# One transpose for two heads in the recurrence, and the place of the half sums ahead of the feed-forward

## The chip, the cores and the metric

The kernel runs on one core of one Trainium2 chip. The metric is the device time of one execution in microseconds. Its engines work beside each other, each in the order of its own queue: TensorE (PE, with its weight loads PEld) multiplies and transposes, VectorE (DVE) and ScalarE (ACT) do elementwise work and read the results out of PSUM, GpSimd (POOL) does small work, and SyncE (SP) issues the transfers.

## The reference

One encoder layer is applied to 512 sample tokens and to 256 prompt tokens of width 1024. It is a mixer, a cross attention and a feed-forward, each with a norm before and after it and a residual:

```python
x = x + rms_norm(hybrid_mixer(rms_norm(x, p['g_mix_pre']), p), p['g_mix_post'])
m = rms_norm(mem, p['g_mem'])
x = x + rms_norm(cross_attention(rms_norm(x, p['g_x_pre']), m, p), p['g_x_post'])
h = rms_norm(x, p['g_ffn_pre'])
x = x + rms_norm(jnp.square(jax.nn.relu(h @ p['w_ff1'])) @ p['w_ff2'], p['g_ffn_post'])
```

Half of the mixer is a recurrence over the tokens (RWKV-7), with 8 heads of 64 and both directions; in each step a head's 64x64 state is decayed, corrected and extended:

```python
sa = jnp.einsum('bhij,bhj->bhi', S, -kk_t)
S = (S * w_t[:, :, None, :] + sa[..., None] * (kk_t * a_t)[:, :, None, :]
     + v_t[..., None] * k_t[:, :, None, :])
```

The other half is a gated linear attention in chunks of 64. All arithmetic is float32.

## The kernel before, in words

A float32 number is kept as a high part and a low part, and each product is made of three matmuls (high by high, high by low, low by high). split() (line 145) makes the two parts: ACT copies the high part, and DVE or POOL subtracts it from the number to get the low part. The 768 tokens are 6 tiles of 128.

**The recurrence.** Heads go in 4 pairs p; one head of a pair lies on partitions 0 to 63, the other on 64 to 127. The tokens are 12 chunks of 64, handled in 6 groups g of two chunks in each direction. products(st, g) (line 1001) is called for each pair and group, 24 times in all, and makes what does not depend on the state. It loads b_ (tile bkg), a_, tp and xv, makes the scores sa and sb on PE, masks them on DVE (lines 1021 to 1024), and then turns b_ over: for each of the two heads, four transposes of 64 rows by 128 columns (line 1028, PSUM tile bktp) and one ACT copy into bkt (line 1029). bkt lies in the tiles pl_hh, pl_hl and pl of the profile. PE multiplies it with the new values in line 1066.

step() (line 1035) is one step of the chain of states for two or three groups side by side: PE, ACT, PE, ACT, PE, DVE in turn. stage(q) (line 1160) places steps and the products for later steps beside each other, and the memory's keys and values (memory_block, line 1128, PE lines 249 and 1139) fill PE between them. The scores, bktp and the sums of finish() share the two PSUM banks of psm (line 75, tag "m").

**The passage to the feed-forward.** After the attention's output projection, channels_first(i) (line 1455) norms tile i (line 1458), transposes it (1462), and writes its high half on ACT (1465) and its low half on DVE (1466) into blk[j][l], the half j of the channels by the half l of the tokens (l = 0 is tiles 0 to 2, l = 1 is tiles 3 to 5). evacuate(i) (1434) and residual(i) (1445) come before it: DVE lines 1442 and 1450, ACT lines 1441 and 1452, POOL lines 1262 and 1264, and the stores of the new x to x2d.

The feed-forward multiplies blocks in Strassen's manner, with seven products of halves in place of eight for each of 8 slices f of 512 hidden channels. The right factors are, in the order of the products n, "21", "11", "t1", "t2", "22", "t3", "t4". "11" and the like are blocks as they stand; t1 to t4 are sums and differences of blocks. For these, both() (line 1594) first adds a block's high and low parts into an ordinary float32 tile (hsum, line 1596): four blocks in two parts q, eight instructions. Further differences (sub, line 1488) and splits (lines 149 and 150) follow. The left factors are weights: raw loads (w), sums of weights (ws, lines 1519 and 1488), and get() (line 1530), which makes the high part wh on ACT (1538) and the low part wl on DVE or POOL (1539). Line 1548 is the product on PE, into fz and fx. The order of the first products is slice 0 n 0 and 1, slice 1 n 0 and 1, slice 0 n 2 to 6, slice 1 n 2 to 6.

**What sets the order.** The program is written in the order of the code, and a planner (schedule_with_timeline_sim, line 1767) orders each engine's instructions before the run: of what is ready by its own model, that which has the highest priority, which is the place in the code unless tc.high_priority raises it. It hands out PSUM banks and tile buffers in the same pass. order_after(ins, prev) (line 43) tells it that one instruction must stand behind another, with no semaphore between them. Transfers are all issued by SP in order.

Of the kernel before, what the change touches and what calls it, by code (L numbers as in the profile page):

```python
# [10 lines left out]
AF = mybir.ActivationFunctionType  # L11
ALU = mybir.AluOpType
# [20 lines left out]
def kernel(ctx: ExitStack, tc: tile.TileContext, I, y_prompt, y_sample):  # L33
    nc = tc.nc
    act = nc.scalar
    dve = nc.vector
    pool = nc.gpsimd
    pe = nc.tensor
# [4 lines left out]
    def order_after(ins, prev):  # L43
        if prev is not None:
            tc.add_manual_dep(
                ins.ins,
                prev.ins.name,
                mybir.DependencyInfo(mybir.DependencyClass.NoSync, mybir.DependencyReason.DATA),
                reason="psum group order",
            )  # L50
        return ins

# [22 lines left out]
    def psm(name):  # L75
        return ps.tile([P, 512], F32, tag="m", bufs=2, name=name)
# [22 lines left out]
    ident = cp.tile([P, P], F32, name="ident")  # L99
# [28 lines left out]
    def fl(ap):  # L128
        return ap.rearrange("p a b -> p (a b)")
# [5 lines left out]
    HS = (slice(0, 64), slice(64, 128))  # L135
# [224 lines left out]
    def small_part(i, part):  # L360
# [6 lines left out]
        if part != 1:  # L367
# [7 lines left out]
                      in1=cv[:, col["mu_next"]:col["mu_next"] + 16], op=ALU.add)  # L375
# [112 lines left out]
    if True:  # L488
# [72 lines left out]
        with tc.high_priority(offset=3000):  # L561
            for p in range(4):
# [15 lines left out]
                for c0, n in SEQS:  # L578
                    pt, pz = psy("lops"), psy("gzps")
# [16 lines left out]
        for i in range(4):  # L596
# [3 lines left out]
            for k0 in range(0, KD, 4):  # L600
                pt = psm("ptr")
# [399 lines left out]
    def products(st, g):  # L1001

        p = st["p"]
        xv, a_, bkt, rbk, tp = places[g]
        b_ = mq1.tile([P, 4, 2, 64], F32, tag="bkg", bufs=3, name="bkg")
        dma(b_, bkd[p][:, g])
        for h, hs in enumerate(HS):
            dma(a_[hs, :, h:h + 2, :].rearrange("p u i x -> p u (i x)"), ard[p][hs, g])
        dma(tp, ttd[p][:, g])
        a, b = g, BACK[g]  # L1010
        for h in range(2):
            dma(xv[HS[1 - h], h].rearrange("p (d c) x -> p d (c x)", c=2),
                vtd[p][h][:, a:b + 1 if b > a else b - 1 if b else None:b - a])
        sa = psm("sca").rearrange("p (u x) -> p u x", u=4)
        sb = psm("scb").rearrange("p (u x) -> p u x", u=4)
        for u in range(4):
            pe.matmul(out=sa[64:128, u, :], lhsT=b_[0:64, u, 1, :], rhs=fl(a_[0:64, u, 0:2, :]), start=True, stop=True)
            pe.matmul(out=sb[0:64, u, :], lhsT=b_[64:128, u, 0, :], rhs=fl(a_[64:128, u, 1:3, :]), start=True, stop=True)
            pe.matmul(out=sa[0:64, u, 64:128], lhsT=b_[0:64, u, 0, :], rhs=a_[0:64, u, 1, :], start=True, stop=True)
            pe.matmul(out=sb[64:128, u, 0:64], lhsT=b_[64:128, u, 1, :], rhs=a_[64:128, u, 1, :], start=True, stop=True)  # L1020
        dve.tensor_tensor(out=u2(a_[64:128, :, 0, :]), in0=u2(sa[64:128, :, 0:64]), in1=bc2(m_strict[64:128]), op=ALU.mult)
        dve.tensor_tensor(out=u2(rbk[:, :, 0:64]), in0=u2(sa[:, :, 64:128]), in1=bc2(m_incl), op=ALU.mult)
        dve.tensor_tensor(out=u2(a_[0:64, :, 2, :]), in0=u2(sb[0:64, :, 64:128]), in1=bc2(m_strict[0:64]), op=ALU.mult)
        dve.tensor_tensor(out=u2(rbk[:, :, 64:128]), in0=u2(sb[:, :, 0:64]), in1=bc2(m_incl), op=ALU.mult)
        for h in range(2):
            pt = psm("bktp")[:, 0:256].rearrange("p (c x) -> p c x", c=4)
            for u in range(4):
                pe.transpose(out=pt[:, u, :], in_=fl(b_[HS[h], u]), identity=ident[HS[h], HS[h]])  # L1028
            act.activation(out=bkt[:, :, h, :], in_=pt, func=AF.Copy)

    def at_step(x, j):

# [170 lines left out]
    order = (4, 5, 6, 7, 0, 1, 2, 3)  # L1203
# [51 lines left out]
        return pd  # L1255

    CS = (slice(0, 512), slice(512, D))

    def rstd(sp, ss):

# [72 lines left out]
    with tc.tile_pool(name="ao", bufs=1, reuse_waits="tile") as ao:  # L1333
# [18 lines left out]
        for h in range(4):  # L1352
# [16 lines left out]
            for s_, (c0, n) in enumerate(SEQS):  # L1369
# [19 lines left out]
                for m in range(2):  # L1389
                    pt = psm("xt")  # L1390
# [4 lines left out]
                for e in range(2):  # L1395
# [3 lines left out]
                                     for m in range(2)])  # L1399
                    act.activation(out=oh[:, 2 * h + e, c0:c0 + n], in_=pm[:, 0:n], func=AF.Copy)  # L1400
                    dve.tensor_tensor(out=ol[:, 2 * h + e, c0:c0 + n], in0=pm[:, 0:n], in1=oh[:, 2 * h + e, c0:c0 + n],
                                      op=ALU.subtract)
# [5 lines left out]
        blk = [[[hb.tile([P, 4, 384], F32R, name=f"h{x}{j}{l}") for x in "hl"] for l in range(2)] for j in range(2)]  # L1408
        with tc.tile_pool(name="op2", bufs=1, reuse_waits="tile") as op2:
            wo2 = load_rows(op2, I["wo_x"][0], 1, range(KD))  # L1410

            def gain_half(name, half, tag):
                g_ = op2.tile([P, 512], F32, tag=tag, name="ghalf")
                dma(g_, I[name][:, CS[half]].broadcast_to([P, 512]))
                return g_

            g_post = [gain_half("g_x_post", 0, "gA"), gain_half("g_x_post", 1, "gB")]
            g_pre = [gain_half("g_ffn_pre", 0, "gC")]
            mo0, sums = [], []
            for i in range(6):  # L1420
                ts_ = slice(i * P, (i + 1) * P)
                pd = (psd, psy)[i % 2]("po")
                mm3(pd, [((oh[:, k, ts_], ol[:, k, ts_]), wo[k]) for k in range(KD)])
                ss = op2.tile([P, 2], F32, tag="ss2", bufs=6, name="ss2")
                mo = op2.tile([P, 512], F32, tag="mo0", bufs=6, name="mo0")
                with tc.high_priority():
                    act.activation(out=mo, in_=pd, func=AF.Square, scale=1.0 / 32, accum_out=ss[:, 0:1])
                    dve.tensor_tensor(out=mo, in0=pd, in1=g_post[0], op=ALU.mult)
                mo0.append(mo)
                sums.append(ss)  # L1430
            g_pre.append(gain_half("g_ffn_pre", 1, "gA"))
            mos, ress, rss = {}, {}, {}

            def evacuate(i):
                ts_ = slice(i * P, (i + 1) * P)
                res = ress[i] = op2.tile([P, D], F32, tag="res", bufs=2, name="res")
                dma(res, x1d[ts_, :])
                mo = mos[i] = mo0[i], op2.tile([P, 512], F32, tag="mo1", bufs=2, name="mo1")
                pd = (psd, psy)[i % 2]("po")
                mm3(pd, [((oh[:, k, ts_], ol[:, k, ts_]), wo2[k]) for k in range(KD)])  # L1440
                act.activation(out=mo[1], in_=pd, func=AF.Square, scale=1.0 / 32, accum_out=sums[i][:, 1:2])
                dve.tensor_tensor(out=mo[1], in0=pd, in1=g_post[1], op=ALU.mult)
                rss[i] = rstd(op2, sums[i])

            def residual(i):
                ts_ = slice(i * P, (i + 1) * P)
                mo, res = mos[i], ress[i]
                ss = op2.tile([P, 2], F32, tag="ss3", bufs=2, name="ss3")
                for half, cs in enumerate(CS):
                    dve.scalar_tensor_tensor(out=res[:, cs], in0=mo[half], scalar=rss[i], in1=res[:, cs], op0=ALU.mult, op1=ALU.add)  # L1450
                    dma(x2d[ts_, cs], res[:, cs])
                    act.activation(out=mo[half], in_=res[:, cs], func=AF.Square, scale=1.0 / 32, accum_out=ss[:, half:half + 1])
                rss[i] = rstd(op2, ss)

            def channels_first(i):
                mo, res = mos[i], ress[i]
                for half, cs in enumerate(CS):
                    dve.scalar_tensor_tensor(out=mo[half], in0=res[:, cs], scalar=rss[i], in1=g_pre[half],
                                             op0=ALU.mult, op1=ALU.mult)
                    pt = psm("ptr")  # L1460
                    for k in range(4):
                        pe.transpose(out=pt[:, k * P:(k + 1) * P], in_=mo[half][:, k * P:(k + 1) * P], identity=ident)
                    pt = pt.rearrange("p (k x) -> p k x", k=4)
                    hi, lo = (x[:, :, i % 3 * P:i % 3 * P + P] for x in blk[half][i // 3])
                    act.activation(out=hi, in_=pt, func=AF.Copy)
                    dve.tensor_tensor(out=lo, in0=pt, in1=hi, op=ALU.subtract)

            evacuate(0)
            for i in range(6):
                residual(i)  # L1470
                if i < 5:
                    evacuate(i + 1)
                channels_first(i)
# [12 lines left out]
    with tc.tile_pool(name="f1", bufs=1, reuse_waits="tile") as f1, tc.tile_pool(name="fw", bufs=1, reuse_waits="tile") as fw:  # L1486
# [98 lines left out]
        h = {"11": blk[0][0], "21": blk[1][0], "22": blk[1][1], "t1": blk[0][1]}  # L1585
# [3 lines left out]
        fl32 = {}  # L1589
        for q in range(2):  # L1590
            ks = slice(2 * q, 2 * q + 2)
            for ij, (j, l) in {"12": (0, 1), "11": (0, 0), "22": (1, 1), "21": (1, 0)}.items():
                fl32[ij, q] = stage_tile({"12": "a", "11": "b", "22": "c", "21": "d"}[ij] + str(q), "hsum")
        def both(q, ij, j, l):
            ks = slice(2 * q, 2 * q + 2)
            dve.tensor_tensor(out=fl32[ij, q], in0=blk[j][l][0][:, ks, :], in1=blk[j][l][1][:, ks, :], op=ALU.add)
        def halves_of(t, q, src, lo_eng):
            ks = slice(2 * q, 2 * q + 2)
            split(h[t][0][:, ks, :], h[t][1][:, ks, :], src, lo_eng)
# [18 lines left out]
        for at, (f, n) in enumerate(jobs):  # L1618
# [29 lines left out]
            if n in (1, 4, 5):  # L1648
                u = st[{1: "11", 4: "12", 5: "22"}[n]]
# [121 lines left out]
```

## Time and profile before

| | us |
|---|---|
| median of 3 timed runs | 1554.85 |
| the three runs | 1558.52, 1554.85, 1549.77 |
| the profiled execution | 1548.75 |
| its span, first to last instruction | 1546.6 |
| PE busy on the transposes of bktp (192) | 21.8 |
| DVE on the sums of the halves (8), mean of one | 0.95 |

A row of the timeline gives the start and length in us, the engine, the line, the operation, what it writes and reads, the shape and the number of instructions; in square brackets stands how long the engine was idle before it and what ended that wait. A row of the groups gives the same without a start, then the busy time in us and the mean of one in ns, then the idle time before them. Matmuls overlap, so their lengths don't add up; what one takes from the queue is seen in the starts of its neighbours.

### The profile page before, as it was taken

Reading aid. Unit: us, or ns where it says so; the run is one execution under the profiler, and the core shown is the slowest. Engines: PE = TensorE matmul, PEld = TensorE weight load, DVE = VectorE, ACT = ScalarE, POOL = GpSimd, SP = SyncE. Lnnn points to the kernel's source line nnn. Section 1 sums busy time; section 2 is a strip of 40 time slices with the busy share of each in tenths; the row PEclk is TensorE's granted clock in tenths of the full one; section 3 lists DMA queues with packets and bytes.
Section 4 is the critical chain, followed back from the end, with each engine's and each line's share of the span. In section 5 each row is a group of like instructions: output and inputs, shape, how many; then the busy total and the mean of one; then the engine's idle time right before and its main releaser. Section 6 shows DMA issues by size and latency. Waiting matters only on the chain.

```text
span 1546.6 us, 27578 instructions
## 1 busy us (share of the span) xinstructions
PE 1408.3 (91%) x10238; PEld 1183.6 (77%) x10238; DVE 1076.7 (70%) x1913; ACT 706.0 (46%) x1477; POOL 220.9 (14%) x304
## 2 busy tenths in 40 slices
PE   7998899897799987999699999978999999999996
PEld 6886778775676766777478887868999998787785
DVE  5555896698567994866665554279766667788886
ACT  5664345443423442344353454345554555454342
POOL 5301000000000000003211233320000002132132
PEclk9999899987779996799799999988999999999998
DMA  6687666584468667464452332244554547555334
GB/s 165 177 314 210 171 197 156 167 228 102 128 187 232 180 184 168 106 166 144 128 179 98 107 100 79 82 154 155 196 170 153 181 157 291 155 175 172 120 103 136
DMA packets 279562, 250.30 MB, mean 162 GB/s; under 512 B 89264, under 2 KB 227059, under 8 KB 279428
## 3 DMA queue, kind: packets, MB, share of 16 engines
q1 hardware_dynamic: 279428, 248.54, 53.8%
q8 instruction: 81, 1.33, 0.4%
q14 instruction: 53, 0.43, 0.1%
HBM read 164.11 MB, written 82.58 MB: 160 GB/s over the span
## 4 chain that ended last, share of the span: by engine, by line
PE 59%; DVE 13%; DMA 11%; issue 8%; SPq 3%; ACT 3%; POOL 2%; DVEq 0%; ACTq 0%; POOLq 0%
PE pd L249 19%; PE fx L1548 7%; PE gx L1548 6%; PE fz L1548 5%; PE gz L1548 5%; SPq L41 3%; PE po L249 3%; DMA wraw<-in_w_in_dram 1%; DVE ws L1488 1%; PE hsum L639 1%; DVE wl L1539 1%; DMA raw<-in_w_out_dram 1%; PE xo L249 1%; POOL rs L1264 1%; PE bktp L1028 1%
## 5 line engine op out<-in xcount | busy, mean ns | idle before, releaser
L249 PE MATMUL pd<-hT_hi,whi 128*128 128x256 f32 (+1 forms) x512 | 183.5, 358 | 9.1 <-DVE gd L327 4.1
L249 PE MATMUL pd<-hT_lo,whi 128*128 128x256 f32 (+1 forms) x512 | 180.2, 352 | 0.3 <-DVE hT_lo L208 0.3
L249 PE MATMUL pd<-hT_hi,wlo 128*128 128x256 f32 (+1 forms) x512 | 178.5, 350 | 0.0
L149 ACT ACTIVATE whi<-wraw 128x256 fp32r<-128x256 f32 x192 | 77.5, 415 | 97.2 <-PE pd L249 59.4
L249 PEld LDWEIGHTS pd<-hT_hi,whi 128*128 128x128 f32 x512 | 100.9, 197 | 24.0 <-DVE gd L327 4.0
L150 DVE TENSOR_TENSOR wlo<-wraw,whi 128x256 fp32r<-128x256 f32 x192 | 80.2, 437 | 48.2 <-ACT whi L149 46.6
L249 PEld LDWEIGHTS pd<-hT_lo,whi 128*128 128x128 f32 x512 | 101.0, 197 | 13.1 <-DVE hT_lo L208 0.5
L249 PEld LDWEIGHTS pd<-hT_hi,wlo 128*128 128x128 f32 x512 | 100.2, 196 | 13.2 <-issue 0.5
L150 DVE TENSOR_TENSOR ul<-ur,uh 128x768 fp32r<-128x768 f32 x56 | 75.3, 1351 | 30.2 <-ACT uh L149 17.7
L149 ACT ACTIVATE uh<-ur 128x768 fp32r<-128x768 f32 x56 | 47.2, 845 | 106.6 <-PE gz L1548 51.8
L1538 ACT ACTIVATE wh<-w 128x1024 fp32r<-128x1024 f32 x64 | 67.1, 1053 | 36.7 <-PE fz L1548 24.2
L1539 DVE TENSOR_TENSOR wl<-w,wh 128x1024 fp32r<-128x1024 f32 x56 | 68.2, 1217 | 15.3 <-ACT wh L1538 14.7
L1548 PE MATMUL gx<-wh,uh 128*128 128x512 f32 x192 | 74.9, 397 | 4.2 <-DVE acc L1741 4.2
L1548 PE MATMUL gx<-wl,uh 128*128 128x512 f32 x192 | 75.9, 395 | 0.0
L1548 PE MATMUL gx<-wh,ul 128*128 128x512 f32 x192 | 75.4, 395 | 0.0
L1539 POOL TENSOR_TENSOR wl<-w,wh 128x1024 fp32r<-128x1024 f32 x8 | 20.9, 2610 | 329.3 <-ACT wh L1538 329.3
L1548 PE MATMUL fz<-hh,wh 128*128 128x384 f32 x192 | 66.1, 344 | 1.7 <-ACT wh L1538 1.7
L1548 PE MATMUL fz<-hl,wh 128*128 128x384 f32 x192 | 65.9, 343 | 0.0
L1548 PE MATMUL fz<-hh,wl 128*128 128x384 f32 x192 | 65.2, 344 | 0.6 <-DVE wl L1539 0.6
L1538 ACT ACTIVATE wh<-ws 128x1024 fp32r<-128x1024 f32 x48 | 50.5, 1052 | 27.2 <-PE fx L1548 22.5
L1548 PE MATMUL gz<-wl,uh 128*128 128x512 f32 x144 | 56.9, 395 | 0.0
L249 PE MATMUL pd<-mem_hi,wlo 128*128 128x512 f32 x128 | 56.0, 439 | 0.9 <-DVE wlo L150 0.9
(537 smaller groups left out, 3980.4 us busy)
## 6 DMA issues: line engine op xcount, KB each, us to landing
w<-in_w_ff_dram SPq DMA_DIRECT2D x64, 512.0 KB
ur<-ud SPq DMA_DIRECT2D x56, 384.0 KB
wraw<-in_w_in_dram SPq DMA_DIRECT2D x108, 128.0 KB
ud<-u SPq DMA_DIRECT2D x32, 384.0 KB
ud<-us SPq DMA_DIRECT2D x24, 384.0 KB
wraw<-in_wkv_x_dram SPq DMA_DIRECT2D x64, 128.0 KB
lora<-lo_t SPq DMA_DIRECT2D x20, 384.0 KB
bkg<-bkd SPq DMA_DIRECT2D x24, 256.0 KB
```

The source lines that it names most:

```text
L41: return nc.sync.dma_start(out=out, in_=in_)
L149: act.activation(out=hi, in_=src, func=AF.Copy)
L150: (lo_eng or pool).tensor_tensor(out=lo, in0=src, in1=hi, op=ALU.subtract)
L249: pe.matmul(out=out, lhsT=a, rhs=b, start=(i == 0), stop=(i == n - 1))
L639: pe.matmul(out=pt[:, 0:n], lhsT=ones_bd, rhs=src[:, c0:c0 + n], start=True, stop=True)
L1028: pe.transpose(out=pt[:, u, :], in_=fl(b_[HS[h], u]), identity=ident[HS[h], HS[h]])
L1264: pool.tensor_tensor(out=rs, in0=ms, in1=neg_half, op=ALU.pow)
L1488: dve.tensor_tensor(out=out, in0=a, in1=b, op=ALU.subtract)
L1538: act.activation(out=hi, in_=t[name], func=AF.Copy)
L1539: lo_eng.tensor_tensor(out=lo, in0=t[name], in1=hi, op=ALU.subtract)
L1548: pe.matmul(out=out, lhsT=a, rhs=b, start=first and i == 0, stop=last and i == n - 1, skip_group_check=True)
```

## The change

In products() the two heads' transposes become one of all 128 rows for each u, into the whole PSUM tile, and one copy takes the place of two. In the passage to the feed-forward the last instruction of line 1466 is remembered, and each of the eight sums of line 1596 is told to stand behind it on DVE. As channels_first goes through the tiles in order, what is remembered is the low half of the last tile's second half of channels. The words given as a reason are renamed.

```diff
-        for h in range(2):
-            pt = psm("bktp")[:, 0:256].rearrange("p (c x) -> p c x", c=4)
-            for u in range(4):
-                pe.transpose(out=pt[:, u, :], in_=fl(b_[HS[h], u]), identity=ident[HS[h], HS[h]])
-            act.activation(out=bkt[:, :, h, :], in_=pt, func=AF.Copy)
+        pt = psm("bktp").rearrange("p (u x) -> p u x", u=4)
+        for u in range(4):
+            pe.transpose(out=pt[:, u, :], in_=fl(b_[:, u]), identity=ident)
+        act.activation(out=bkt.rearrange("p u h x -> p u (h x)"), in_=pt, func=AF.Copy)
...
+    last_lo = [None]
...
-                    dve.tensor_tensor(out=lo, in0=pt, in1=hi, op=ALU.subtract)
+                    last_lo[0] = dve.tensor_tensor(out=lo, in0=pt, in1=hi, op=ALU.subtract)
...
-            dve.tensor_tensor(out=fl32[ij, q], in0=blk[j][l][0][:, ks, :], in1=blk[j][l][1][:, ks, :], op=ALU.add)
+            order_after(dve.tensor_tensor(out=fl32[ij, q], in0=blk[j][l][0][:, ks, :], in1=blk[j][l][1][:, ks, :],
+                                          op=ALU.add), last_lo[0])
```

More of the change, by code (lines that the diff above doesn't have):

```diff
@@ L48, in order_after @@
                 mybir.DependencyInfo(mybir.DependencyClass.NoSync, mybir.DependencyReason.DATA),
-                reason="psum group order",
+                reason="order",
             )
```

## The prediction

> **What bounds the kernel now.** I read the page first, then stage tables for the two places that the change touches, then the timelines, groups and waits there.
>
> ```profile
> span 1546.6 us, 27578 instructions
> ## 1 busy us (share of the span) xinstructions
> PE 1408.3 (91%) x10238; PEld 1183.6 (77%) x10238; DVE 1076.7 (70%) x1913; ACT 706.0 (46%) x1477; POOL 220.9 (14%) x304
> ```
>
> TensorE (PE) is busy for 91% of the span. So an edit pays where it shortens PE's own queue, or where PE stands waiting. The stage tables show one place of each kind; the columns are stage, length, busy time of PE, weight loads, VectorE (DVE), ScalarE (ACT) and GpSimd, then granted clock, DMA share and GB/s.
>
> ```profile
> 430.00:760.00 330.00, 297.22 (x3772) 228.26 (x3770) 239.52 (x628) 121.20 (x333) 14.55 (x29) 0.87 0.62 167
> 600.00:630.00 30.00, 27.15 (x366) 22.56 (x364) 22.39 (x72) 7.17 (x23) 0.00 (x0) 0.50 0.68 174
> 1031.00:1050.00 19.00, 6.74 (x24) 4.98 (x24) 16.51 (x22) 8.48 (x15) 1.72 (x4) 0.58 0.64 204
> 1050.00:1081.00 31.00, 28.36 (x141) 27.79 (x140) 31.00 (x33) 15.85 (x22) 0.00 (x0) 0.87 0.36 110
> ```
>
> The recurrence, where all 24 calls of products() run, is 430 to 760: PE works 297.22 of 330 us (90%), so time taken from its queue there is mostly worth its face value. The passage from the last norm to the feed-forward is 1031 to 1050: PE works 6.74 of 19 us while DVE works 16.51. From 1050 to 1081 DVE works every microsecond and PE loses another 2.6 us. So the passage belongs to DVE.
>
> **Part 1, the transposes.** Gone are 192 transposes of 64 rows and 48 evacuations of 128x256; new are 96 transposes of 128 rows and 24 evacuations of 128x512. The nearest row for the new transpose is line 1139, which moves four 128x128 blocks in the same stretch. The start of the next group in the timeline gives what each takes from the queue.
>
> ```profile
> 474.88 0.56 PE L1028 MATMUL bktp<-ident,bkg 64*128 64x64 f32 x8
> ...
> 690.22 0.47 PE L1028 MATMUL bktp<-ident,bkg 64*128 64x64 f32 x8
> 690.62 0.50 PE L249 MATMUL pd<-mem_hi,wlo 128*128 128x512 f32 x1
> ...
> 706.52 0.66 PE L1139 MATMUL kvt<-ident,mo 128*128 128x128 f32 x4
> 707.11 0.32 PE L1046 MATMUL rec<-pl_hh 64*64 64x64 f32 x2
> 707.36 0.46 PE L1028 MATMUL bktp<-ident,bkg 64*128 64x64 f32 x4
> 707.75 0.45 PE L1077 MATMUL rec<-pl 128*64 128x64 f32 x8
> ```
>
> One head's four transposes take 707.75 - 707.36 = 0.39 us of the queue, so a pair done one head after the other takes 0.78. Eight in one group take 690.62 - 690.22 = 0.40: there the heads overlapped. The new group takes 707.11 - 706.52 = 0.59. So a product whose heads stand apart gains 0.19 us, and one whose heads overlap loses 0.19. In PE's timeline three of the 24 products overlap like this (the first at 474.88, the last at 690.22); in the others the heads stand apart or run one after the other. That makes 21 x 0.19 - 3 x 0.19 = 3.4 us less in PE's queue; times the 90%, 3.1 us.
>
> The Trainium skill (TensorE: Matmul & The Clock Gate, Part 3: Packing small matmuls) says that matmuls on different row groups of the array run at the same time, and the two heads sit on rows 0 to 63 and 64 to 127. By that rule all 24 products would overlap already, part 1 would be 0.9 x 24 x 0.19 = 4.1 us lost, and the sum below 1555.95. The groups of eight agree with it; the groups of four show that the heads rarely stand side by side in the queue.
>
> ```profile
> L1029 ACT ACTIVATE pl_hh<-bktp 128x256 f32<-128x256 f32 x16 | 5.8, 384 | 8.6 <-PE bktp L1028 8.1
> ...
> L1142 ACT ACTIVATE mo<-kvt 128x512 f32<-128x512 f32 x8 | 4.8, 596 | 2.3 <-PE kvt L1139 2.2
> ```
>
> ```profile
>   PEld rec L1051: 1.3, 3
>   PEld sca L1017: 1.0, 2
>   PEld rec L1066: 0.8, 1
>   PEld bktp L1028: 0.7, 1
> ```
>
> On ACT, 48 x 0.384 = 18.4 us become 24 x 0.596 = 14.3 us. ACT works 121 of 330 us there, so those 4.1 us are hidden behind PE either way; if ACT were the bound they would come on top. The second fence is what PE's weight loads waited for behind line 1029 (us in total, times): 3.8 us. Its last row is the second head waiting for the first head's evacuation, which goes for good (0.7). The others stay: the last copy is now 0.596 - 0.384 = 0.21 us longer, but there is one instead of two. I take 0.7 of the 3.8. Fewer holds on the two "m" banks could shorten PE's waits for DVE's reads of sca and scb; I count nothing for that, since those waits end when DVE has read the scores, before any transpose. Sum of part 1: 3.1 + 0.7 = 3.8, of which I keep 3.0, because some PE time freed inside a recurrence step only uncovers the next wait of that step. Bounds: all heads apart and all waits gone, 24 x 0.19 + 3.8 = 8.4 us gained; all heads overlapped already, 24 x 0.19 = 4.6 us lost.
>
> **Part 2, the sums of the halves.** The eight sums of line 1596 may stand on DVE only behind the last tile's last low half (line 1466). Before, six stood ahead of it:
>
> ```profile
> 1030.87 0.95 DVE L1596 TENSOR_TENSOR hsum<-hh,hl 128x768 f32<-128x768 f32 x1
> 1031.74 0.69 DVE L1466 TENSOR_TENSOR hl<-ptr,hh 128x512 fp32r<-128x512 f32 x1
> 1032.34 2.68 DVE L1596 TENSOR_TENSOR hsum<-hh,hl 128x768 f32<-128x768 f32 x3
> ...
> 1039.96 1.41 DVE L1458 SCALAR_TENSOR_TENSOR mo<-res,rs,ghalf 128x512 f32<-128x512 f32 x2 [1.22 <-POOL rs L1264]
> 1042.61 0.69 DVE L1466 TENSOR_TENSOR hl<-ptr,hh 128x512 fp32r<-128x512 f32 x1 [1.24 <-ACT hh L1465]
> 1043.34 1.83 DVE L1596 TENSOR_TENSOR hsum<-hh,hl 128x768 f32<-128x768 f32 x2
> 1045.08 0.69 DVE L1466 TENSOR_TENSOR hl<-ptr,hh 128x512 fp32r<-128x512 f32 x1
> ...
> 1049.15 1.22 DVE L1539 TENSOR_TENSOR wl<-w,wh 128x1024 fp32r<-128x1024 f32 x1
> ```
>
> Back to back one takes 0.87 us (1031.74 - 1030.87), so 6 x 0.87 = 5.2 us leave the last norm's path: four stand ahead of that tile's evacuation and residual, two before its last low half. What PE then waits for is the first weights' low half (line 1539, 1049.15):
>
> ```profile
> 1050.42 0.69 PE L1548 MATMUL fz<-hh,wl 128*128 128x384 f32 x1 [0.21 <-DVE wl L1539]
> ...
> 1075.40 0.69 PE L1548 MATMUL fx<-t2h,wl 128*128 128x384 f32 x1 [2.43 <-DVE wl L1539]
> ```
>
> PE's first products could start up to 5.2 us sooner. The weight loads move too: SyncE issues them in order behind the last tile's two stores to x2d, which wait for the residual that the four sums delay by 4 x 0.87 = 3.5 us; so the raw weights come that much sooner and don't take the cover away. But the 5.2 us come back on DVE after the norm, where it has no free time until 1081, and behind them stand the sums' own users (the products with t1 to t4) and the weights' splits. If all that DVE does before the wait at 1075.40 ends is needed by then, PE only waits more there and the gain is nothing; if the norm's gaps, so far filled by sums, stay empty besides, it is a loss. The norm's two idle gaps in the fence (1.22 and 1.24) are 2.5 us together; doubled, the loss is 2.5. If DVE could put off what is not yet due, the gain is 5.2 plus PE's waits of 2.43 and 0.21: 7.8 us. Work that is not yet due stands there:
>
> ```profile
> 1060.31 1.21 DVE L1488 TENSOR_TENSOR ws<-w,w 128x1024 f32<-128x1024 f32 x1
> 1061.44 0.95 DVE L150 TENSOR_TENSOR t3l<-hsum,t3h 128x768 fp32r<-128x768 f32 x1
> 1062.31 1.21 DVE L1519 TENSOR_TENSOR ws<-w,w 128x1024 f32<-128x1024 f32 x1
> ```
>
> The two weight sums are the second slice's (each slice has one of line 1519, and this is the second), used from the tenth product on; t3 is used in the eighth; PE is at its sixth at 1075. These three alone are 3.4 us. Whether the planner puts them behind can't be seen in this trace, so I take 3 us, a little under the middle of 0 and 7.8, because the loss of 2.5 is open too.
>
> **Sum.** The profiled execution took 1548.75 us, its span of 1546.6 and 2.15 around it; 1548.75 - 3.0 - 3.0 = 1542.75. The median of the three timed runs is 1554.85, 6.1 above that execution; carried onto it, the forecast is **1548.85**.
>
> **The rivals.**
>
> *Both gains come nearly whole* (0.27). Heads apart almost everywhere and waits gone, 5 us; DVE puts off what isn't due, 7.8 us. 1554.85 - 12.8 = 1542.05. For it: PE's queue is the bound at both places. Against it: DVE is full for 31 us.
>
> *Nothing is saved* (0.16). The heads overlap in most products and DVE hands the 5.2 us back: 0.9 x 4.6 = 4.1 us lost, nothing gained, 1558.95. For it: a group of eight takes as long as a group of four, and DVE is full. Against it: only three of 24 products show such a group.
>
> *A bare wait in the recurrence* (0.12), the case of slower. The order of the engines is planned afresh, and the products' PE and ACT work is what stands between the steps and the loads.
>
> ```profile
> 586.38 0.21 PE L796 MATMUL merge<-tdz,lsb 32*32 32x32 f32 x2 [4.21 <-DMA tdz<-td]
> ```
>
> Here PE stood 4.21 us for a transfer, and from 600 to 630 the clock was 0.50. At half clock the 27.15 us worked there would have been 13.6 at full clock. One more such place costs 4.2 + 13.6 = 17.8 us; less the 6 gained, 1554.85 + 11.8 = 1566.65. It decides as soon as one wait of over 4 us stands in the recurrence that wasn't there. The Trainium skill (TensorE: Matmul & The Clock Gate, Part 1) gives about 3.4 us as the window after which an idle PE falls to half clock; the 4.21 us wait and the 0.50 agree with it. For this rival: PE's queue is in order, so a merge placed too early holds all that stands behind it. Against it: a shorter queue of products frees banks and ACT rather than binding them.
>
> **How the numbers follow.** The forecast has 0.45, with its own range from 1544 to 1555. A measurement of this kernel can tell about 0.5% (7.8 us) from no change, so faster means under 1547.1 and slower over 1562.6. Faster: the first rival's 0.27 and 0.11 of the forecast's, 0.38. Slower: the last rival, 0.12. Within: 0.50. The range goes down to 1538, where parts 1 and 2 at their best bounds (8.4 + 7.8 = 16.2 under the median) put it, and up to 1561.5, which takes in the second rival and a further 2.5 us lost on DVE, and leaves out most of the last rival.
>
> **What would show it.** Right: PE's transposes of bktp become 24 groups of 0.66 us, 16 us in all; ACT's on line 1029 to 14.3; all eight sums stand behind the last line 1466, which ends near 1040.5 if the recurrence kept its length; line 1548 takes up its wl products some 5 us sooner after the last out-projection, and DVE's waits in front of it grow between the fourth and the seventh product. Wrong: the feed-forward's continuous stretch begins as late after the last out-projection as before; the recurrence's length moves by over 8 us either way, which would be its new order and not the transposes; or its clock changes.

## The result, and the profile after

| | before | after |
|---|---|---|
| median, us (18 runs each) | 1554.93 | 1564.72 |
| lowest and highest | 1548.71 to 1567.42 | 1558.04 to 1570.67 |
| profiled execution | 1548.75 | 1566.52 |
| its span | 1546.6 | 1564.6 |

The change makes the kernel slower: the ratio is 1.0053, with a 95% interval of 1.0032 to 1.0074, some 8 us. Two numbers have to be kept apart. The profiled execution of before lies 6 us under that kernel's median, the one of after 2 us above its own. So differences between the two traces show where time went, but their sum, 18 us, is about twice what the medians show; sizes are taken from the ratios.

The page of after, to hold against the page lines of before:

```profile
span 1564.6 us, 27338 instructions
...
PE 1408.3 (90%) x10142; PEld 1182.4 (76%) x10142; DVE 1079.6 (69%) x1913; ACT 701.0 (45%) x1453; POOL 224.5 (14%) x304
```

PE's busy time is 1408.3 us in both kernels. Nothing is worked longer; PE stands idle longer. The stages of after, with the passage to the feed-forward shifted by 19 us, because the last output projection ends at 1049.0 in place of 1030.1 (same columns as in the prediction):

```profile
430.00:760.00 330.00, 289.29 (x3558) 222.51 (x3557) 235.85 (x610) 111.34 (x294) 18.09 (x29) 0.86 0.60 164
600.00:630.00 30.00, 28.03 (x480) 23.06 (x479) 18.23 (x58) 10.64 (x29) 0.00 (x0) 0.89 0.75 187
680.00:730.00 50.00, 38.23 (x536) 31.13 (x536) 19.04 (x52) 10.74 (x26) 0.00 (x0) 0.55 0.48 124
1050.00:1069.00 19.00, 8.18 (x30) 6.53 (x31) 16.99 (x23) 9.37 (x16) 1.69 (x4) 0.58 0.78 250
1069.00:1100.00 31.00, 27.59 (x145) 26.96 (x144) 31.00 (x32) 15.69 (x21) 0.00 (x0) 0.93 0.30 93
```

In the recurrence PE works 289.29 of 330 us, 8 less than before; the half clock that stood at 600 to 630 is gone from there (0.89) and stands at 680 to 730 (0.55). The passage is much as it was. So the loss lies in the recurrence, and both parts of the change did what they say. The groups of bktp in after (count, then shortest, median and longest in ns, first and last start):

```profile
L1027 PE MATMUL bktp<-ident,bkg x96: 270/273/476, 441.6 to 754.9; 128*128 128x128 f32 x96
L1028 ACT ACTIVATE pl_hh<-bktp x8: 592/597/597, 442.8 to 717.5; 128x512 f32<-128x512 f32 x8
```

The transposes are 96 of 128 rows, and a copy takes 0.597 us, as forecast from line 1142. The sums in after, on DVE:

```profile
1058.34 0.69 DVE L1466 TENSOR_TENSOR hl<-ptr,hh 128x512 fp32r<-128x512 f32 x1 [0.16 <-ACT hh L1465]
1058.95 7.03 DVE L1596 TENSOR_TENSOR hsum<-hh,hl 128x768 f32<-128x768 f32 x8
1065.89 1.22 DVE L1539 TENSOR_TENSOR wl<-w,wh 128x1024 fp32r<-128x1024 f32 x1
```

and what PE then waits for:

```profile
1067.16 0.69 PE L1548 MATMUL fz<-hh,wl 128*128 128x384 f32 x1 [4.63 <-DVE wl L1539]
```

All eight sums stand behind the last low half, in one block of 7.03 us, and the first weights' low half stands behind all of them: PE waits 4.63 us for it where it waited 0.21.

Where does the recurrence lose its time? SP's queue shows it. Before, the rows of the third pair's inverses and join (td<-snf is a store of the inverses, tdz<-td what the join loads from it, sxf<-ld the load for the fourth pair's inverses):

```profile
576.72 0.83 SPq L41 DMA_DIRECT2D td<-snf  x1
...
579.51 2.14 SPq L41 DMA_DIRECT2D td<-snf  x1
...
590.26 1.04 SPq L41 DMA_DIRECT2D tdz<-td  x1
...
602.50 0.71 SPq L41 DMA_DIRECT2D sxf<-ld  x1
```

After:

```profile
576.05 0.33 SPq L41 DMA_DIRECT2D td<-snf  x1
...
582.31 0.88 SPq L41 DMA_DIRECT2D tdz<-td  x2
...
601.36 0.46 SPq L41 DMA_DIRECT2D td<-snf  x1
...
602.92 1.41 SPq L41 DMA_DIRECT2D sxf<-ld  x1
...
606.70 0.91 SPq L41 DMA_DIRECT2D tdz<-td  x2
```

The second store goes out at 601.36 in place of 579.51. DVE had its data ready at 578.3, as before (578.5). The copy that makes it, before and after:

```profile
577.33 1.12 DVE L760 COPY snf<-sqf 48x1024 f32<-48x1024 f32 x1
```

```profile
577.23 1.08 DVE L760 COPY snf<-sqf 48x1024 f32<-48x1024 f32 x1
```

In after the store stands behind 11 transfers that are a weight's and the join's own, to 585.7, and then behind 21 others, 13 of them loads for later products(). The join's second half needs it, and its results lie in the tile (sqf) that the fourth pair's inverses clear first. PE's second half of the join and DVE's first step of the fourth pair's inverses, before:

```profile
592.71 0.94 PE L796 MATMUL merge<-tdz,lsb 32*32 32x32 f32 x46 [0.78 <-DMA tdz<-td]
```

```profile
613.11 0.19 DVE L752 TENSOR_TENSOR stmp<-sqf,snf 112x31 f32<-112x31 f32 x1
```

and after:

```profile
610.03 1.66 PE L796 MATMUL merge<-tdz,lsb 32*32 32x32 f32 x48 [1.43 <-DMA tdz<-td]
```

```profile
626.91 0.18 DVE L752 TENSOR_TENSOR stmp<-sqf,snf 112x31 f32<-112x31 f32 x1
```

The inverses then end at 673 in place of 646, and the fourth pair's join and all of the recurrence that hangs on it come later. The later start is 14 of these 27 us. The other 13 are length: between the inverses' first and last step DVE does 24.3 us of other work in the new order, where it did 15.0. On the way stands a wait that is much easier to see. SP sends a result of the late inverses (sxf) at 685.95; ACT's square in finish() reuses that buffer; PE stands behind ACT:

```profile
685.95 0.78 SPq L41 DMA_DIRECT2D qd<-sxf  x1
```

```profile
690.87 0.84 ACT L1105 ACTIVATE fb<-ya 128x768 f32<-128x768 f32 x1 [10.73 <-DMA qd<-sxf]
```

```profile
691.77 2.93 PE L639 MATMUL hsum<-fb,ones_bd 128*128 128x512 f32 x4 [11.25 <-ACT fb L1105]
```

No wait points at the store: from 579 to 601, where the loss begins, PE's longest is 2.62 us, shorter than the 4.21 us in the same place before. The waits of the recurrence show only the loss's end.

### The profile page after: what moved, and what is told of

Its sections match the earlier page's. It is cut to its first block, busy times and chain, and to the rows that moved or that the text cites. A ratio compares the mean times of both kernels' runs of the same rounds, so it can differ in the third digit from the quotient of the medians.

```text
span 1564.6 us, 27338 instructions
## 1 busy us (share of the span) xinstructions
PE 1408.3 (90%) x10142; PEld 1182.4 (76%) x10142; DVE 1079.6 (69%) x1913; ACT 701.0 (45%) x1453; POOL 224.5 (14%) x304
## 4 chain that ended last, share of the span: by engine, by line
PE 59%; DVE 16%; DMA 8%; issue 8%; ACT 4%; SPq 3%; POOL 2%; DVEq 0%; POOLq 0%; ACTq 0%
PE pd L249 18%; PE fx L1548 7%; PE gx L1548 6%; PE gz L1548 5%; PE fz L1548 5%; PE po L249 3%; SPq L41 3%; DVE ws L1488 1%; DVE wl L1539 1%; PE xo L249 1%; PE sca L1017 1%; PE hsum L639 1%; DVE wlo L150 1%; PE xs L249 1%; POOL rs L1264 1%
## 5 line engine op out<-in xcount | busy, mean ns | idle before, releaser
L1548 PE MATMUL gz<-wh,ul 128*128 128x512 f32 x144 | 56.6, 395 | 0.0
```

The lines of the kernel that those rows point to most:

```text
L1548: pe.matmul(out=out, lhsT=a, rhs=b, start=first and i == 0, stop=last and i == n - 1, skip_group_check=True)
```

## The experiments

Each ratio is to before, from runs on the same chip. The milestones, in us, come from the traces: when the last store of the third pair's inverses is issued; the first and last step (line 752) of the fourth pair's inverses; the last product of its join (line 808); the last output projection of the mixer, behind which all kernels differ only in part 2.

| kernel | ratio, 95% interval | store | inverses | join | mixer |
|---|---|---|---|---|---|
| before | 1 | 579.5 | 613.1 to 646.3 | 673.5 | 844.8 |
| after | 1.0053 [1.0032, 1.0074] | 601.4 | 626.9 to 672.8 | 709.9 | 860.9 |
| e1, part 1 alone | 1.0057 [1.0024, 1.0090] | 598.1 | 620.8 to 666.9 | 699.2 | 851.5 |
| e2, part 2 alone | 0.9945 [0.9914, 0.9976] | 588.1 | 620.5 to 653.7 | 678.7 | 855.1 |
| e3, after, own scratch | 1.0018 [0.9987, 1.0050] | 599.9 | 624.4 to 670.4 | 709.1 | 859.4 |
| e4, before, own scratch | 1.0115 [1.0072, 1.0158] | 584.8 | 617.4 to 650.5 | 678.0 | 870.3 |
| e5, 4 blocks held | 0.9994 [0.9963, 1.0024] | 603.6 | 627.0 to 661.6 | 690.5 | 860.3 |
| e6, 2 blocks held | 0.9970 [0.9941, 1.0000] | 598.4 | 623.2 to 665.1 | 692.1 | 850.0 |
| e7, before, transposes first | 1.0032 [0.9997, 1.0066] | 579.1 | 614.4 to 656.1 | 689.2 | 849.3 |
| e8, after, two copies | 0.9952 [0.9920, 0.9984] | 577.7 | 610.7 to 656.0 | 687.6 | 843.0 |
| e9, after, store early | 0.9972 [0.9944, 1.0000] | 584.7 | 611.1 to 657.2 | 692.7 | 851.0 |
| e10, before, store late | 1.0109 [1.0072, 1.0147] | 603.7 | 625.1 to 664.9 | 701.4 | 861.9 |
| e11, after, stores first | 0.9997 [0.9977, 1.0016] | 581.2 | 613.6 to 646.9 | 676.2 | 850.7 |
| e12, two copies, stores first | 0.9915 [0.9881, 0.9949] | 585.4 | 617.7 to 652.5 | 676.2 | 842.9 |

The milestones belong to one execution each; e2's profiled one was the slowest of its twelve, e1's the fastest. Before and e2 share one order up to the mixer's end, after and e1 another, and yet the mixer's end lies some 10 us apart within each of these pairs. So a single milestone is no measure of a gain or a loss of 8 us; the ratios are.

**Each part alone (e1, e2).** e1 is before with the changed lines of products(), e2 is after with the old ones.

> The transposes alone; the sums of the halves stay where they were. Theory A (the time is lost in the recurrence, where the new order of the engines leaves PE waiting 11.25 us for ScalarE's square in finish() and then working 40 us at half clock): slower than before by 14 to 20 us, the last out-projection matmul of the mixer near 860.9 as in the changed kernel against 844.8 before. Theory B (the transposes and the longer copy cost the time themselves): the same total, but PE's busy time or its waits on line 1028's copies grow by most of it; they did not in the changed kernel's trace. Theory C (the moved sums cost the time): within 3 us of before.

> The moved sums alone; the transposes stay two per pair. Theory A: the recurrence's order is that of before to the end of the mixer, and the norm's tail is about 2 us shorter, of which VectorE hands back about 1; the attention, whose order changes too, may cost up to 3: in all -2 to +3 us. Theory C: slower by 9 us or more. My forecast of -3 for this part: 1551 to 1553.

Part 1 alone loses as much as the whole change, 9 us where theory A expected 14 to 20, and the wait for the square stands there too (12.6 us). Part 2 alone gains, 9 us where -2 to +3 were expected. The order of the whole recurrence in e2 is before's, the store included.

**The wait that is seen (e3, e4).** finish() gets a scratch tile of its own for the first three pairs, so that it need not wait for sxf; e3 does that to after, e4 to before.

```diff
+    fp_cm = tc.tile_pool(name="fp", bufs=1, reuse_waits="tile")
+    fp = fp_cm.__enter__()
...
-        finish(sts[0])
+        finish(sts[0], tiles=(fp.tile([P, T], F32, tag="fb", name="fb"),) * 3)
```

> The changed kernel, but the scratch tile of finish() for the first three pairs lies in the room that the memory's tiles left, not in the tile that the fourth pair's inverse still sends out from. The planned order is that of the changed kernel up to that square and differs behind it. Theory A: PE's wait of 11.25 us at 680 is gone and with it most of the half clock from 680 to 723; the time falls by 10 to 20 us below the changed kernel, to between 1545 and 1555. Rival D (the matmuls of the memory's keys and values, which fill PE between the steps, are used up by 660 in place of 707, so the recurrence's rest is bare whatever is waited for): the wait goes elsewhere, the clock still falls, and less than 6 us come back.

> The kernel before with the same own scratch tile and nothing else. The room that the memory's tiles leave comes free only after the last of their matmuls, at 707 before. Theory A: the tile held nothing up before, so within 5 us of before, either way. If it gains 8 us or more, the own tile is worth that in any order, and its gain in the changed kernel doesn't speak for the wait at 680.

In e3 the wait of 11.25 us is gone, and the ratio falls from 1.0053 to 1.0018, some 5 us and not the 10 to 20 expected: the fourth pair's join still comes at 709.1. That is what rival D expected, and the intervals of after and e3 overlap. In e4 the same edit costs 18 us, which nothing of what was expected covers; the scratch tile changes the order everywhere. Two later runs say more: e6 has the same wait, 14.43 us of it, and stands at 0.9970; e10 has no wait of PE above 3.2 us there and stands at 1.0109. So the largest wait in the trace of after is an effect, and the theory that it was the cause falls.

**The memory blocks that fill PE (e5, e6).** In after, the matmuls of memory_block(), which fill PE between the steps, are used up at 660, 50 us before the join; before, they last to 707. e5 and e6 order the last four, or two, of the 16 blocks behind the join's last product.

```diff
-    for b in range(16):
+    for b in range(14):
         memory_block(mem, b)
-    mq2_cm.__exit__(None, None, None)
...
     joined(3)
+    for b in range(14, 16):
+        memory_block(mem, b, last_join[0])
+    mq2_cm.__exit__(None, None, None)
```

> The changed kernel, but the matmuls of the last 4 of the 16 memory blocks may stand on PE only behind the last matmul of the fourth pair's join. Theory D (the new order uses up the memory's matmuls, which fill PE between the steps, by 654 to 660, while the fourth pair's inverse, join and products are still to come; before, they lasted to 707): PE's busy share in 680 to 720 rises from 28 to over 34 us, the inverse and the join come sooner, and the time falls 8 to 18 us below the changed kernel, to 1545 to 1556. Theory B (the transposes and copies themselves cost it): no change beyond 4 us.

> The same with 2 memory blocks held back instead of 4. Theory D: part of that gain, 3 to 10 us below the changed kernel; the planned place of the inverse on VectorE doesn't move with only two, so if the inverse's place is what counts and not the filler, nothing. Theory B: no change.

Both take back the loss, 9 to 13 us, with the store as late as in after, and in both the memory's matmuls last past the join (to 757 and 734). Theory D expected that. The next pair shows that the fillers alone don't decide.

**The order alone, and the copy (e7, e8).** e7 is before's own instructions, with the transposes and their copies written ahead of the scores. e8 is after with two copies of 128x256 in place of one:

```diff
-        act.activation(out=bkt.rearrange("p u h x -> p u (h x)"), in_=pt, func=AF.Copy)
+        for h in range(2):
+            act.activation(out=bkt[:, :, h, :], in_=pt[:, :, h * 64:h * 64 + 64], func=AF.Copy)
```

> The kernel before with the very same instructions, but in products() the transposes and their two copies are written ahead of the scores. The planned order then looks like that of the changed kernel: the fourth pair's inverse later on VectorE and the last join behind the last memory block. Theory D (the order alone costs it): slower than before by 6 to 16 us, though no transpose is merged. Theory B: within 4 us of before.

> The changed kernel with the four transposes of 128 rows, but two ScalarE copies of 128x256 in place of one of 128x512. This too gives another order, with the last memory block ahead of the last join, as in the changed kernel. Theory D: slower than before by 4 to 14 us, near the changed kernel. If the longer single copy were the cost (a form of theory B): back to within 3 us of before, or faster.

e7 is some 5 us slower than before with before's own instructions, 1.0032, but its interval just reaches no change. e8 is faster than before, though its memory blocks run out at 656, as in after; theory D expected it 4 to 14 us slower. So blocks that run out early do not by themselves make the loss. e8 is also what was expected if the long single copy were the cost; the next pair excludes that, as e9 gains with the single copy and e10 loses without it. What sets e8 apart from after is that its third pair's second store goes out at 577.7. In e1, e3, e5 and e6 that store is as late as in after.

**The store, both ways (e9, e10).** e9 is after with one ordering added: the next loads of the recurrence stay behind the store.

```diff
-        dma(td[1].rearrange("s b c t -> (b c) s t"), sn[64:112])
+        sto[st["p"]] = dma(td[1].rearrange("s b c t -> (b c) s t"), sn[64:112])
...
+        first = sto[2] if (p, g) in ((1, 2), (1, 3), (2, 0), (2, 4)) else None
...
-            dma(a_[hs, :, h:h + 2, :].rearrange("p u i x -> p u (i x)"), ard[p][hs, g])
-        dma(tp, ttd[p][:, g])
+            order_after(dma(a_[hs, :, h:h + 2, :].rearrange("p u i x -> p u (i x)"), ard[p][hs, g]), first)
+        order_after(dma(tp, ttd[p][:, g]), first)
```

e10 is before with the opposite: the store behind the last load (vt) of the third pair's first group.

```diff
-            dma(xv[HS[1 - h], h].rearrange("p (d c) x -> p d (c x)", c=2),
+            vt[p, g] = dma(xv[HS[1 - h], h].rearrange("p (d c) x -> p d (c x)", c=2),
...
+    order_after(sto[2], vt[2, 0])
     joined(3)
```

> The changed kernel, with one ordering added: on SyncE's queue the loads of A, R and T for the next groups of the recurrence (groups 2 and 3 of the second pair, 0 and 4 of the third) stay behind the last store of the third pair's inverses, instead of that store standing behind 15 of them. Every engine's order is the changed kernel's own up to that store. Theory S (the late store is the loss: it delays the second half of the third pair's join from 592.7 to 610.0 us, with it the fourth pair's inverses from 613 to 627, and with them the fourth pair's join and the mixer's end by 16 us): the store is issued by 582, the second half of the join by 597, the inverses start at 613 to 618 and end at 655 to 662 in place of 673.8, the mixer ends 8 to 14 us earlier, and the time is 0.995 to 0.999 of before's (8 to 15 us below the changed kernel's 1.0053). Rival F (the memory blocks, which the changed order uses up before the join, decide, and the store only goes with them): they still run out early here, so within 4 us of the changed kernel, 1.003 to 1.008.

> The kernel before, unchanged in every instruction, with the one ordering turned round: the last store of the third pair's inverses stands on SyncE's queue behind the loads of the third pair's first group, as it does in the changed kernel. Every engine's order is that of before up to that store. Theory S: the second half of the third pair's join comes at 605 to 612 us in place of 592.7, the fourth pair's inverses start at 622 to 630 in place of 613.1, and the time is 8 to 16 us longer than before's, 1.005 to 1.010. Rival F, and any theory that puts the loss on the transposes or on the copy: nothing of these is changed, so within 4 us of before, 0.997 to 1.003.

SP's queue in e9:

```profile
584.72 0.46 SPq L41 DMA_DIRECT2D td<-snf  x1
...
589.61 0.81 SPq L41 DMA_DIRECT2D tdz<-td  x2
...
601.51 1.14 SPq L41 DMA_DIRECT2D sxf<-ld  x1
```

and in e10:

```profile
603.74 0.42 SPq L41 DMA_DIRECT2D td<-snf  x1
604.22 0.72 SPq L41 DMA_DIRECT2D sxf<-ld  x1
...
608.99 0.79 SPq L41 DMA_DIRECT2D tdz<-td  x2
```

In e9 every engine's order is after's own until that store; the one edit turns 1.0053 into 0.9972, 12.6 us of 1555. In e10 every engine's order is before's own until there; the edit turns 1 into 1.0109, 17 us (11 to 23 by its interval), where 8 to 16 were expected. The first steps of the fourth pair's inverses move with it, e9 and then e10:

```profile
611.06 0.18 DVE L752 TENSOR_TENSOR stmp<-sqf,snf 112x31 f32<-112x31 f32 x1
```

```profile
625.05 0.19 DVE L752 TENSOR_TENSOR stmp<-sqf,snf 112x31 f32<-112x31 f32 x1
```

The theory of the store holds from both sides: 13 and 17 us hang on the place of one transfer and on what the planner orders behind it, with and without the change. e9 is the cleaner of the two, as its memory blocks run out at 657, much as in after; in e10 they run out at 673 where before's last to 707, so rival F isn't excluded there. And a late store does not cost by itself: in e5 and e6 it is as late, and they are no slower than before. In after, e1, e3 and e10, the store is late and the memory blocks are used up 27 us or more before the fourth pair's join; in e5 and e6 they last past it. So the loss seems to need both, a late join and nothing left to fill PE until then. That reading fits all these runs, but no run was made to test it. One number in e9's expectation is off: of the transfers that the store stood behind, 13 and not 15 were the recurrence's.

**Stores ahead of everything (e11, e12).** The stores of all inverses get the join's priority, four each in e11 (on after), the two to td in e12 (on e8).

```diff
-        dma(td[1].rearrange("s b c t -> (b c) s t"), sn[64:112])
+        with tc.high_priority(offset=6000):
+            dma(td[1].rearrange("s b c t -> (b c) s t"), sn[64:112])
```

> The changed kernel with the four stores of every pair's inverses given the join's own priority (6000) in place of 2000, so that none is put behind the loads of the recurrence; the order changes from the second pair's inverses on. The memory blocks last past the join here, as in before, and the fourth pair's inverses take 98 rows of VectorE's order, as in before, not 112. Theory S with the fillers on top: 0.992 to 0.998 of before's time. Rival F alone would give as much, but it then must also show the changed kernel's time in the run above where the store alone is moved. A theory that puts the loss on the 128-row transposes or the single 128x512 copy: 1.002 to 1.008.

> The changed kernel with two copies of 128x256 behind the four transposes (the run that stood at 0.9952 of before) and, on top, the last two stores of every pair's inverses at priority 6000. The third pair's store is early without it, so theory S expects no gain from that pair; the fourth pair's join comes 65 rows earlier in TensorE's order and the memory blocks last past it. Theory S: 0.992 to 0.997. Rival F (fillers beyond the join are worth the 10 us that the changed kernel lost): 0.988 to 0.992.

e11 is a miss: its join and inverses are as early as before's, and it gains nothing on before. Its order differs from after's from the second pair on, and what it loses again is not found. e12 is the best kernel of the study, 0.9915, some 13 us under before. That lies in the range of rival F and just under that of theory S; its interval reaches into both. Its join (676.2) comes early and its memory blocks last past it (to 700.4), so the fillers can have a share in what it has over e8. The intervals of e8 and e12 overlap, and the runs don't divide it further.

## Why the prediction was wrong

- **The step that failed** is the one that lies under the whole sum: that the recurrence keeps its order, so that part 1 is worth what it takes from PE's queue. The text named the other case, "the order of the engines is planned afresh", and gave it 0.12. That rival's time, 1566.65, is within 2 us of the measured median, and its place is right, but its mechanism is not, so that the number fits is luck. It has PE stand for a transfer because a product was placed too early, and adds one more stretch of half clock. In fact one store was placed too late on SP's queue, by 22 us; PE lost little there, and stood idle only 80 us on, with the fillers used up. Putting the store back (e9) took back 12.6 us. The half clock was not one more: that of 600 to 630 went, and one at 680 came. Nor did the wait of 4.21 us bring the half clock that the rival prices with it: from 590.5 to 593.5 the granted clock was 1.00 again, and when it fell to 0.50 again at 594, PE had waited 0.78 us at most since that long wait. The prediction's own sign of being wrong, a recurrence that changes its length by over 8 us, is what came.
- **Part 1** itself is near its forecast. PE's busy time on bktp falls from 21.8 to 19.1 us in the groups, 2.7, against 3.4 from the starts of neighbours; 19.1 is more than the 16 that the text named. One reading under the 3.4 is wrong: not three but at least five products had their heads overlapped in before (at 474.88, 485.20, 561.31, 635.25 and 690.22, eight transposes in 0.40 to 0.49 us), which gives 19 x 0.19 - 5 x 0.19 = 2.7. The copies are as forecast. With the store early (e9), the whole change stands at 0.9972, 4.3 us gained with an interval from 0 to 8.7, against the 6.0 forecast: the sum agrees with that, but the interval is too wide to confirm it. The trace of before had rows on the order (the store at 579.51), but none on how near the planner was to turning it.
- **Part 2** came out at its size. From the mixer's last output projection to the end of the span, the five kernels with the old sums take 705.2 us on average, the nine with the new ones 702.2, with a spread (standard deviation) of 2.0 in either set: 3.0 us, which is the forecast. From the start of the attention's last output projection, nearer to where the part begins, it is 517.7 against 514.3, 3.4 us, with spreads of 0.8 and 1.1. Its steps are only in part right: the first product with wl starts 18.1 to 18.2 us behind that projection in all nine, in place of 20.3 to 20.4 in all five, so 2.2 of the 5.2 us arrive at once, and DVE's sums keep the rest; the planner did not put off all eight sums but set them ahead of the first wl. e2's 0.9945 is more than 3 us; its interval reaches down to 3.7, and what lies between is not explained.
- **"Nothing is saved"** expected heads that overlap anyway. e1 at 1.0057 looks like it, but e8 and e9 keep the same transposes and are 16 and 13 us under after, so that was not it.
- **The range** ended at 1561.5 and left the last rival out; the median of 1564.72 is that rival's.

Why the planner moves the store is not settled. With the transposes of after, one copy puts it late and two copies do not; with before's transposes written first it stays early. Kernels with the store in the same place still differ (e7 and e9, whose inverses run 42 and 46 us in place of 33, while DVE does 24.2 and 22.8 us of other work between their steps, not 15.0), and e5 and e6 make up for a late store.

## What to carry to other kernels

Where a planner sets the order, a small edit is priced in two sums: what it saves, and what the new order does; the second was here up to three times the first, and of either sign. Look for the second in the issue order of the queues and not among the longest waits: compare, in both traces, when each store goes out with when its data was ready, and see whether the work that fills the idle engine lasts until then. Then pin that one transfer, in both kernels, before judging the edit; here that turned a loss of 0.5% into a gain of 0.3%, whose interval just reaches no change. Two copies in place of one made it 0.5 to 0.9%.

## What the runs showed that was not expected

- The store's data lay ready for 23 us while SP had its turn elsewhere: the last 21 transfers ahead of it took SP from 585.80 to 601.36, 0.7 us each. The Trainium skill (DMA: Bandwidth & Descriptors, Rules for kernel authors) says that spreading transfers over several issuing engines saves only issue time. No run here tried that; the trace shows that other transfers' issue time alone held this store back.
- The half clock does not follow PE's longest wait. In after it falls at 677.4, while PE still works, 3 us before the wait of 11.25 us begins, and it outlasts that wait, which ended at 691.77: from 700 to 720 PE worked all of every 10 us, and the clock was still 0.50 (columns as in the stage tables):

```profile
677.00:680.00 3.00, 2.83 (x44) 2.35 (x46) 2.02 (x8) 0.95 (x4) 0.00 (x0) 0.57 0.71 149
680.00:690.00 10.00, 0.52 (x8) 0.33 (x8) 0.87 (x3) 0.14 (x1) 0.00 (x0) 0.50 0.65 121
690.00:700.00 10.00, 8.23 (x133) 6.09 (x134) 2.42 (x5) 3.83 (x7) 0.00 (x0) 0.50 0.43 93
700.00:710.00 10.00, 10.00 (x161) 8.38 (x161) 4.78 (x9) 2.35 (x6) 0.00 (x0) 0.50 0.43 145
710.00:720.00 10.00, 10.00 (x112) 8.47 (x109) 4.64 (x13) 2.46 (x7) 0.00 (x0) 0.50 0.65 187
```

  In e9 the clock is as low in the same place, though PE has no wait above 2.6 us from 663 to 753:

```profile
680.00:720.00 40.00, 37.34 (x476) 30.22 (x476) 18.21 (x51) 7.34 (x21) 0.00 (x0) 0.53 0.52 156
```

  The Trainium skill (TensorE: Matmul & The Clock Gate, Part 1) gives about 3.4 us of sustained work until the full clock returns. Here it took over 20 us, so the measurement differs from the page.
- Runs of one kernel spread by 19 us (before: 1548.71 to 1567.42), twice the effect that was measured; with 18 runs of each the interval is still 0.2% to either side, and with the six of e4, e10 and e12 some 0.4%. The spread goes with the granted clock: of the runs of before beside e1 to e4, one took 1546.42 us at a mean clock of 0.931 and one 1567.81 us at 0.917. Kernels differ in it too. Over its runs, after has 0.930 and before, beside the experiments, 0.925 to 0.927, so the change is not slower for its clock. But e8 and e12 have 0.936 and e10 0.920: a part of their distance from before may be the clock's, and the runs don't tell whether their order makes the clock.
